# Five raw weight buffers in place of three, and a smaller scratch for software DMAs, in an fp32 encoder layer on one core

## The chip, the core and the metric

The kernel runs on one core of one Trainium2 chip. Its engines are TensorE (PE in the profile; PEld is its weight loads), VectorE (DVE), ScalarE (ACT), GpSimd (POOL) and SyncE (SP), which here only issues DMAs. Each engine works through its own queue in order and waits at semaphores. The metric is the device time of one execution in microseconds. Before the change the median of three runs is 819.6 us (819.17 to 819.94).

## The reference

One layer of an encoder, 512 tokens of width 1024, all in float32:

```python
D_MODEL = 1024; SEQ = 512; D_FF = 2752
def swiglu(h, w_gate, w_up, w_down):
    return (jax.nn.silu(h @ w_gate) * (h @ w_up)) @ w_down
...
    x = x + 0.5 * swiglu(rms_norm(x, ffn1_norm), ffn1_w_gate, ffn1_w_up, ffn1_w_down)
    h = rms_norm(x, mix_norm)
    u = h @ w_in
    ...
    f_out = fourier_mixer(u[..., :o0], fnet_w, fnet_b)
    a_out = gqa_attention(u[..., o0:o1], u[..., o1:o2], u[..., o2:], q_norm, k_norm)
    x = x + jnp.concatenate([f_out, a_out], axis=-1) @ w_out
    x = x + 0.5 * swiglu(rms_norm(x, ffn2_norm), ffn2_w_gate, ffn2_w_up, ffn2_w_down)
return rms_norm(x, final_norm)
```

The two feed-forward blocks (FFN1 and FFN2) hold most of the work: three weight matrices of 1024 x 2752 each. The mixer between them has a Fourier part and an attention part.

## The kernel before

**Arithmetic.** TensorE multiplies in fp32r, a rounded float32. To keep float32 accuracy each operand is split into a high part (a cast) and a low part (what the cast lost), and a product is three matmuls: high by high, high by low, low by high (`product`, L186). For weights the high part is cast by ScalarE (`weights`, L172; `both`, L391; `single`, L400) and the low part is a subtraction on VectorE (`lows`, L130), from the raw tile and the high part. A few low parts are made by GpSimd's software DMA, which adds the weights from memory onto the negated high part (`rest_by_dma`, L159 and L160).

**Tiles.** Activations stand transposed: eight tiles of 128 features by 512 tokens. The feed-forward width is cut into 21 chunks of 128 and a rest (`"t"`). A block is done in four groups of chunks (`GROUPS1`, `GROUPS2`). Gate and up of a chunk are computed in one of two ways. In the first group they are plain products (`gate`). In the others a 2 x 2 block scheme with seven products in place of eight is used (`seven`, with p, q and r as its PSUM banks); it needs sums of raw gate and up weights, which `prepare` makes: s12 and s34, four VectorE operations (`combine`, L406) of 128x512, cast and split afterwards as 128x1024. After gate and up of a group, `down` multiplies the group's activations (tile at) with the down weights for each of eight output tiles d (dn0_d_g: FFN 0 or 2, tile d, group g), and `residual` (L575) adds half of it to the residual stream gx. A group of six chunks gives 18 matmuls per d, one of two or three chunks with the rest some 8 to 11.

**Buffers.** Weights come from memory as raw tiles of 4 KB per partition. Down weights (`raw_tile`, L154), up weights of `prepare` (raw_u, L383) and the weights of the mixer share one tag "raw" in the pool `wp` (L92), which has three buffers. Gate weights of `prepare` (raw_g) have two buffers in another pool. A load can be issued when the last reader of the tile that had the buffer is done, and SyncE issues the loads in a fixed order, so a load that waits holds up those behind it.

**What sets the order.** On TensorE and SyncE the order inside the feed-forward blocks is that of the program (`in_order`). On VectorE, ScalarE and GpSimd it is set there by the framework's scheduler when the program is built: it simulates the program with its own costs, and so with the buffers that it has. In the mixer all engines follow a list written out by hand (`ORDER`). The profile's time has no part in any of this.

The lines that matter:

```python
def lows(lo, src, hi):                                             # L130
    nc.vector.tensor_tensor(out=lo, in0=src, in1=asf(hi), op=ALU.subtract)
def raw_tile(src, name, n=KD):                                     # L154
    raw = wp.tile([P, KD, P], F32, tag="raw", name=f"raw_{name}")
    nc.sync.dma_start(out=raw[:, :n, :], in_=src)
...
    u = wp.tile([P, KD * P], F32, tag="raw", name=f"raw_u{n_}_{j}")  # prepare
...
    def combine(out, a, b, op):                                    # L406
        nc.vector.tensor_tensor(out=out, in0=a, in1=b, op=op)
```

Of the kernel before, what the change touches and what calls it, by code (L numbers as in the profile page):

```python
# [88 lines left out]
def encoder(ctx, tc, A, out):  # L89
    nc = tc.nc  # L90
    cp = ctx.enter_context(tc.tile_pool(name="const", bufs=1))
    wp = ctx.enter_context(tc.tile_pool(name="weights", bufs=3))  # L92

    whole = cp.tile([P, FRONT + NS * KD * P + 2 * ROOM], F32R, name="ring")
    ring = whole[:, FRONT:]
# [1471 lines left out]
```

## Time and profile before

| | |
|---|---|
| median of three runs | 819.6 us |
| the profiled execution: span | 817.3 us |
| TensorE busy | 809.9 us, 99% |
| VectorE busy | 652.0 us, 80% |
| ScalarE busy | 503.5 us, 62% |
| GpSimd busy | 67.7 us, 8% |
| mean granted TensorE clock | 0.999 |
| moved by DMA | 99.75 MB, 122 GB/s |

The span is that of the profiled execution on the chip, from its first to its last instruction; a run's time is 2.3 us longer at the median, and no other time of that execution is recorded. Times of events are counted from the span's start. FFN1 runs from 0 to some 330, the mixer until some 485, FFN2 until some 810, and the final normalisation is the end. Rows of the timeline are: start, duration, engine, line, operation, what is written from what, shape, and in brackets the idle time before and what ended it. A row of a wait has the engine and line that waited, what it waited for, the total, the count and the longest. A matmul's duration contains its pipeline, so the pace of TensorE is read from starts.

### The profile page before, as it was taken

The numbers are of one execution on the slowest core, as the hardware profiler recorded it, in microseconds if no ns is written. First come the engines' busy times: TensorE is split into PE (matmuls) and PEld (weight loads), VectorE is DVE, ScalarE is ACT, GpSimd is POOL, SyncE is SP. The second block draws the span as 40 slices with busy tenths as digits, with TensorE's granted clock in tenths as the row PEclk, the third lists the DMA queues.
The fourth block names the chain that finished last, engine by engine and source line by source line (L and its number), as shares of the span: only waits on it lengthen the run. The fifth ranks groups of instructions, "written<-read, shape, count | busy, mean of one in ns | idle before, by whom it ended". The sixth has DMA issues, their size and how long they took to land.

```text
span 817.3 us, 13006 instructions
## 1 busy us (share of the span) xinstructions
PE 809.9 (99%) x4936; PEld 729.0 (89%) x4936; DVE 652.0 (80%) x1080; ACT 503.5 (62%) x870; POOL 67.7 (8%) x75
## 2 busy tenths in 40 slices
PE   9999999999999999999999999999999999999997
PEld 6888998899989998889998888899988998899987
DVE  7997997489956857799998578999955997489674
ACT  7883774167624735699998449557733674267462
POOL 0320000000000000221000003100100000000001
PEclk9999999999999999999999999999999999999999
DMA  7874553345443423442201236564443553345222
GB/s 258 199 176 165 146 133 91 123 130 168 85 142 96 126 69 117 130 149 65 66 26 52 79 105 144 128 191 140 132 116 115 154 140 84 129 130 146 59 78 103
DMA packets 37390, 99.75 MB, mean 122 GB/s; under 512 B 4432, under 2 KB 10576, under 8 KB 37328
## 3 DMA queue, kind: packets, MB, share of 16 engines
q1 hardware_dynamic: 27776, 82.61, 31.3%
q0 software_dynamic: 8832, 15.34, 11.1%
q10 hardware_dynamic: 720, 0.98, 0.3%
q8 instruction: 38, 0.62, 0.3%
q14 instruction: 24, 0.20, 0.1%
HBM read 93.41 MB, written 2.10 MB: 117 GB/s over the span
## 4 chain that ended last, share of the span: by engine, by line
PE 96%; DMA 1%; DVE 1%; ACT 1%; issue 0%; POOL 0%; POOLq 0%; DVEq 0%; ACTq 0%
PE dn L186 24%; PE r L436 12%; PE mix L186 8%; PE r L441 8%; PE gu L186 8%; PE q L436 4%; PE q L441 4%; PE r L432 4%; PE p L432 4%; PE q L432 4%; PE gu L740 3%; PE p L441 2%; PE mix L1234 2%; PE mix L1200 2%; PE mix L1038 1%; PE mix L1039 1%
## 5 line engine op out<-in xcount | busy, mean ns | idle before, releaser
L186 PE MATMUL dn<-at,ring 128*128 128x512 f32 x900 | 202.9, 380 | 0.4 <-DVE ring L130 0.4
L186 PEld LDWEIGHTS dn<-at,ring 128*128 128x128 f32 x900 | 168.0, 188 | 29.5 <-DVE ring L130 1.0
L441 PE MATMUL r<-rt,ring 128*128 128x256 f32 x560 | 154.3, 276 | 0.0
L436 PE MATMUL r<-rt,ring 128*128 128x256 f32 x840 | 147.1, 276 | 0.0
L436 PEld LDWEIGHTS r<-rt,ring 128*128 128x128 f32 x840 | 127.0, 188 | 1.6
L441 PEld LDWEIGHTS r<-rt,ring 128*128 128x128 f32 x560 | 105.1, 188 | 0.2
L391 ACT CAST ring<-s 128x1024 fp32r<-128x1024 f32 x70 | 73.6, 1051 | 35.5 <-PE r L436 16.5
L130 DVE TENSOR_TENSOR ring<-s,ring 128x1024 fp32r<-128x1024 f32 x70 | 85.3, 1218 | 12.5 <-ACT ring L391 10.3
L575 DVE SCALAR_TENSOR_TENSOR gx<-dn,gx 128x512 f32<-128x512 f32 x61 | 41.9, 688 | 62.0 <-PE dn L186 61.8
L172 ACT CAST ring<-raw_dn 128x768 fp32r<-128x768 f32 (+3 forms) x58 | 45.3, 784 | 70.5 <-PE dn L186 52.5
L441 PE MATMUL q<-rt,ring 128*128 128x256 f32 x280 | 77.0, 275 | 0.0
L160 POOL DMA_DIRECT2D ring<-in_wgu x38 | 32.9, 867 | 470.9 <-ACT u L450 358.0
L130 DVE TENSOR_TENSOR ring<-raw_dn,ring 128x768 fp32r<-128x768 f32 (+3 forms) x58 | 51.5, 891 | 9.2 <-ACT ring L172 5.1
L441 PEld LDWEIGHTS q<-rt,ring 128*128 128x128 f32 x280 | 52.6, 188 | 0.0
L130 DVE TENSOR_TENSOR ring<-raw_g,ring 128x1024 fp32r<-128x1024 f32 x35 | 42.7, 1220 | 10.0 <-PE p L432 9.6
L436 PE MATMUL q<-rt,ring 128*128 128x256 f32 x280 | 49.8, 277 | 0.0
L186 PE MATMUL gu<-ring 128*128 128x512 f32 x216 | 48.9, 381 | 0.0
L432 PE MATMUL r<-rt,ring 128*128 128x512 f32 x140 | 48.7, 384 | 0.0
L432 PE MATMUL q<-rt,ring 128*128 128x512 f32 x140 | 48.3, 382 | 0.0
L432 PE MATMUL p<-rt,ring 128*128 128x512 f32 x140 | 48.3, 382 | 0.0
L186 PEld LDWEIGHTS gu<-ring 128*128 128x128 f32 x216 | 40.4, 188 | 6.9
L391 ACT CAST ring<-raw_g 128x1024 fp32r<-128x1024 f32 x35 | 36.8, 1051 | 13.9 <-DMA raw_g<-in_wgu 10.9
(277 smaller groups left out, 1658.6 us busy)
## 6 DMA issues: line engine op xcount, KB each, us to landing
raw_g<-in_wgu SPq DMA_DIRECT2D x35, 512.0 KB, 3.8
raw_u<-in_wgu SPq DMA_DIRECT2D x35, 512.0 KB, 4.5
raw_dn<-in_wd SPq DMA_DIRECT2D x40, 384.0 KB, 3.2
ring<-in_wgu POOLq DMA_DIRECT2D x35, 256.0 KB, 4.3
raw_gu<-in_wgu SPq DMA_DIRECT2D x12, 512.0 KB, 3.4
raw_o<-in_wo SPq DMA_DIRECT2D x8, 512.0 KB, 3.5
raw_dn<-in_wd SPq DMA_DIRECT2D x8, 448.0 KB, 3.4
raw_wq<-in_wins SPq DMA_DIRECT2D x4, 512.0 KB, 3.5
```

Of the source, the lines that this page charges most:

```text
L130: nc.vector.tensor_tensor(out=lo, in0=src, in1=asf(hi), op=ALU.subtract)
L160: nc.gpsimd.dma_start(out=lo, in_=src, accum_op=ALU.add)
L172: nc.scalar.copy(hi[:, :n, :], raw[:, :n, :])
L186: nc.tensor.matmul(ps, a, b, start=first and b is mhi and a is whi, stop=last and a is wlo)
L391: nc.scalar.copy(hi, src)
L432: nc.tensor.matmul(turned(ps), whi[:, ks], turned(m), start=start, stop=False, skip_group_check=True)
L436: nc.tensor.matmul(ps[:, t], whi[:, ks], m[:, o * HALF :][:, t], start=start and o == 0, stop=False, skip_group_check=True,)
L441: nc.tensor.matmul(o, wlo[:, ks], m, start=False, stop=stop, skip_group_check=True)
L575: nc.vector.scalar_tensor_tensor(out=x[d][:, t], in0=ps[:, t], scalar=0.5, in1=x[d][:, t], op0=ALU.mult, op1=ALU.add)
L740: nc.tensor.matmul(turned(pss[c]), w[:, k % 2, c], turned(m[k]), start=k == 0 and m is hh and w is hi, stop=k == KD - 1 and w is lo,)
L1200: nc.tensor.transpose(pts[n][:, c * P : (c + 1) * P], prob[t, b, c][:, kc * P : (kc + 1) * P], ident)
L1234: nc.tensor.matmul(turned(outs[t, b]), w, turned(p), start=kc == 0 and i == 0, stop=kc == 3 and i == 1)
```

## The change

The pool of raw weight tiles gets five buffers in place of three, and the scratch that GpSimd's software DMAs use for their descriptors gets 8192 bytes per partition in place of 16384 (the value that holds where none is given):

```diff
@@ encoder
-    wp = ctx.enter_context(tc.tile_pool(name="weights", bufs=3))
+    wp = ctx.enter_context(tc.tile_pool(name="weights", bufs=5))
@@ kernel
-    nc = bacc.Bacc("TRN2", target_bir_lowering=False, num_devices=1)
+    nc = bacc.Bacc("TRN2", target_bir_lowering=False, num_devices=1, dynamic_dma_scratch_size=8192)
```

Two buffers of 4096 bytes take just the 8192 bytes that the scratch gives up. The scratch lies at the start of the memory, so the constant tiles between it and the raw buffers move down by 8192 bytes, and all above the raw buffers stays where it was.

On TensorE and GpSimd the instructions stand as before; SyncE's loads too, but for one at the start that is issued two places earlier. On VectorE and ScalarE the scheduler comes to another order. Three pieces of VectorE's, as a difference (- before, + now; the numbers at the end of a name tell tiles apart).

The first is in FFN1's second group, while TensorE does the down products of d = 1 to 4. raw_dn0_3 to raw_dn0_5 are the down weights for d = 3 to 5, whose low parts are made here; raw_u0_11 and raw_g0_11 are the weights of chunk 11, which the next group needs.

```order
 L130 TENSOR_TENSOR ring_61<-raw_dn0_3_1_1475,ring_61 128x768
 L575 SCALAR_TENSOR_TENSOR gx_69<-dn0_2_1_1449,gx_69 128x512
+L406 TENSOR_TENSOR s12_0_11_1608<-raw_u0_11_1605 128x512
+L406 TENSOR_TENSOR s34_0_11_1609<-raw_g0_11_1604,raw_u0_11_1605 128x512
 L130 TENSOR_TENSOR ring_61<-raw_dn0_4_1_1500,ring_61 128x768
+L406 TENSOR_TENSOR s12_0_11_1608<-s12_0_11_1608,raw_g0_11_1604 128x512
+L406 TENSOR_TENSOR s34_0_11_1609<-raw_g0_11_1604,s12_0_11_1608 128x512
 L575 SCALAR_TENSOR_TENSOR gx_69<-dn0_3_1_1474,gx_69 128x512
 L130 TENSOR_TENSOR ring_61<-raw_dn0_5_1_1526,ring_61 128x768
 L575 SCALAR_TENSOR_TENSOR gx_69<-dn0_4_1_1499,gx_69 128x512
-L406 TENSOR_TENSOR s12_0_11_1608<-raw_u0_11_1605 128x512
-L406 TENSOR_TENSOR s34_0_11_1609<-raw_g0_11_1604,raw_u0_11_1605 128x512
```

The sums of chunk 11 have moved from behind the low part of raw_dn0_5 to both sides of that of raw_dn0_4; all four stand ahead of raw_dn0_5 now. The same is done in FFN1's third group and in the second and third of FFN2.

The second is in FFN2's first group, where at2 is the activations' tile, whose free room also holds a low part of a down weight, and u2p a product of gate and up.

```order
 L130 TENSOR_TENSOR ring_61<-raw_dn2_3_0_5243,ring_61 128x256
-L406 TENSOR_TENSOR s12_2_3_5273<-raw_u2_3_5270 128x512
-L406 TENSOR_TENSOR s34_2_3_5274<-raw_g2_3_5269,raw_u2_3_5270 128x512
+L662 TENSOR_TENSOR u2p_5234<-g2p_5233,u2p_5234 128x512
+L406 TENSOR_TENSOR s34_2_3_5274<-raw_g2_3_5269,s12_2_3_5273 128x512
+L575 SCALAR_TENSOR_TENSOR gx_69<-dn2_1_0_5242,gx_69 128x512
+L130 TENSOR_TENSOR ring_61<-s12_2_3_5273,ring_61 128x1024
+L130 TENSOR_TENSOR at2_4887<-raw_dn2_4_0_5257,at2_4887 128x256
+L575 SCALAR_TENSOR_TENSOR gx_69<-dn2_2_0_5256,gx_69 128x512
 L130 TENSOR_TENSOR at2_4887<-u2p_5234,at2_4887 128x512
-L575 SCALAR_TENSOR_TENSOR gx_69<-dn2_1_0_5242,gx_69 128x512
-L130 TENSOR_TENSOR at2_4887<-raw_dn2_4_0_5257,at2_4887 128x256
```

Ahead of the low part of raw_dn2_4 stand now, beside what stood there, the last sum of s34 for chunk 3 and the 1024-wide low part of its s12; the low part of u2p has moved behind it.

The third is a little later in the same group.

```order
 L575 SCALAR_TENSOR_TENSOR gx_69<-dn2_3_0_5278,gx_69 128x512
-L130 TENSOR_TENSOR ring_61<-s12_2_3_5273,ring_61 128x1024
+L406 TENSOR_TENSOR s12_2_4_5355<-raw_u2_4_5352 128x512
+L130 TENSOR_TENSOR ring_61<-s34_2_3_5274,ring_61 128x1024
 L130 TENSOR_TENSOR ring_61<-raw_dn2_6_0_5294,ring_61 128x256
 L575 SCALAR_TENSOR_TENSOR gx_69<-dn2_4_0_5293,gx_69 128x512
-L130 TENSOR_TENSOR ring_61<-s34_2_3_5274,ring_61 128x1024
 L130 TENSOR_TENSOR at2_4887<-raw_dn2_7_0_5309,at2_4887 128x256
```

The 1024-wide low part of s12 is gone from here, that of s34 has moved ahead of the low part of raw_dn2_6, and with it a sum that reads the up weights of chunk 4.

Other rows moved are the token weights of the last three down tiles at the end of FFN2 (L548, L549: half of a raw tile, split, for products that have tokens as rows), which stand earlier; a sum and a low part in FFN1's first group, which stand ahead of the low part of raw_dn0_5; and the low parts of raw_dn_1, which stand a few rows earlier in four groups.

## The prediction

> **What bounds the kernel now.** I read the page from the top: the busy times, the chain that ended last, then the waits of each engine.
>
> ```profile
> span 817.3 us, 13006 instructions
> PE 809.9 (99%) x4936; PEld 729.0 (89%) x4936; DVE 652.0 (80%) x1080; ACT 503.5 (62%) x870; POOL 67.7 (8%) x75
> PE 96%; DMA 1%; DVE 1%; ACT 1%; issue 0%; POOL 0%; POOLq 0%; DVEq 0%; ACTq 0%
> ```
>
> TensorE (PE) is busy for 99% of the span and carries 96% of the chain. More buffers remove no matmul, so the change can win only what TensorE waits. The waits (engine, line and what was waited for: us in total, times, longest):
>
> ```profile
> PE dn L186 <- DVE ring L130: 0.4, 1, 0.4
> ...
> SPq L154 <- DVE ring L130: 203.7, 46, 13.3
> ```
>
> SyncE's queue stands 203.7 us behind raw buffers that are not free yet, which is what two more of them relax. But that waiting is hidden: TensorE itself waits for a low part in one place that this view shows. The large number is no gain; the small one is. Where that wait comes from stands in the chain (start, us, what):
>
> ```profile
> 147.31 0.97 DVE ring L130
> 148.30 4.86 DMA raw_u<-in_wgu
> 153.79 0.68 DVE s L406
> 154.48 0.88 DVE ring L130
> 155.40 7.75 PE dn L186 x34
> ```
>
> The buffer for the up weights of chunk 11 (raw_u) is freed by the low part of raw_dn5 at 147.31; the load takes until 153.2; VectorE's sums (L406) wait for it, and the low part of raw_dn6 stands behind them on VectorE's queue. That ends at 154.48+0.88 = 155.36, and the matmul that reads it starts at 155.40. How long TensorE stood there is read from the starts:
>
> ```profile
> 139.39 0.96 DVE L130 TENSOR_TENSOR ring<-raw_dn,ring 128x768 fp32r<-128x768 f32 x1
> 153.19 0.69 DVE L406 TENSOR_TENSOR s<-raw_u 128x512 f32<-128x512 f32 x1 [1.87 <-DMA raw_u<-in_wgu]
> ...
> 142.73 12.28 PE L186 MATMUL dn<-at,ring 128*128 128x512 f32 x55
> ```
>
> A 512-wide matmul starts 0.22 us after the one before (further down, three take 530.10 to 530.76). 55 of them from 142.73 put the next at 154.83; it came at 155.40. The wait is 0.57 us.
>
> **The change part by part.** *The stall that goes.* With five buffers that load needs only the low part of raw_dn3, which ends at 139.39+0.96 = 140.35, eight microseconds earlier, and the low part of raw_dn6 no longer has an L406 ahead of it that waits. The term is **-0.57**, and it cannot be more.
>
> *What is late next.* The scheduler has used the earlier load. In four places (the second and third group of each FFN) it puts two of the L406 sums ahead of the low part of raw_dn4, where nothing waited. That low part is due two blocks of 18 matmuls (18 x 0.22 = 3.96 us each) before 154.83, at 146.91. To end 0.04 before that it must start by 146.91-0.04-0.96 = 145.91, and the first of two L406, 0.60 apart (153.19 to 153.79), by 144.71. From an issue at 140.40 that leaves 4.3 us. Before, these rows give the time from the issue of that load to the L406 that waits for it:
>
> ```profile
> 148.30 0.33 SPq L383 DMA_DIRECT2D raw_u<-in_wgu  x1
> 237.49 0.33 SPq L383 DMA_DIRECT2D raw_u<-in_wgu  x1
> 612.01 0.33 SPq L383 DMA_DIRECT2D raw_u<-in_wgu  x1
> 700.51 0.33 SPq L383 DMA_DIRECT2D raw_u<-in_wgu  x1
> ...
> 241.37 0.69 DVE L406 TENSOR_TENSOR s<-raw_u 128x512 f32<-128x512 f32 x1 [0.86 <-DMA raw_u<-in_wgu]
> 615.70 0.69 DVE L406 TENSOR_TENSOR s<-raw_u 128x512 f32<-128x512 f32 x1 [0.67 <-DMA raw_u<-in_wgu]
> 703.97 0.69 DVE L406 TENSOR_TENSOR s<-raw_u 128x512 f32<-128x512 f32 x1 [0.43 <-DMA raw_u<-in_wgu]
> ```
>
> They are 4.89, 3.88, 3.69 and 3.46 us. Three fit into 4.3, one misses by 0.6. The four places together cost between 0 (all in time) and 4 x 0.6 = 2.4 (all as slow as the first). I take **+0.3**, half of one miss, since three of the four rows lie on the side of no wait. Behind the waiting L406 stand, on VectorE, the low part of raw_dn4, two more sums and a residual; only the first of them has TensorE waiting for it.
>
> *The first group of FFN2.* Here it is VectorE that has nothing to spare (its busy time is the fourth figure of the first row, of 20 us):
>
> ```profile
> 520.00:540.00 20.00, 20.00 (x98) 16.85 (x97) 19.55 (x33) 9.19 (x16) 0.92 (x1) 1.00 0.58 189
> ...
> 523.52 1.23 DVE L130 TENSOR_TENSOR ring<-raw_g,ring 128x1024 fp32r<-128x1024 f32 x1 [0.42 <-ACT ring L391]
> 524.66 0.68 DVE L660 TENSOR_TENSOR u2p<-gu,rb 128x512 f32<-128x512 f32 x1
> 532.40 1.21 DVE L130 TENSOR_TENSOR ring<-s,ring 128x1024 fp32r<-128x1024 f32 x1
> 533.53 0.41 DVE L130 TENSOR_TENSOR ring<-raw_dn,ring 128x256 fp32r<-128x256 f32 x1
> 533.87 0.68 DVE L575 SCALAR_TENSOR_TENSOR gx<-dn,gx 128x512 f32<-128x512 f32 x1
> ...
> 530.10 0.82 PE L186 MATMUL dn<-at 128*128 128x512 f32 x3
> 530.76 0.38 PE L533 MATMUL dn<-at,wt 128*128 128x512 f32 x1
> 532.96 1.54 PE L186 MATMUL dn<-at,ring 128*128 128x512 f32 x6
> 534.34 0.39 PE L533 MATMUL dn<-at,wt 128*128 128x512 f32 x1
> 535.45 1.11 PE L186 MATMUL dn<-at 128*128 128x512 f32 x3
> 536.40 0.39 PE L533 MATMUL dn<-at,wt 128*128 128x512 f32 x1
> ```
>
> I laid the new sequence of VectorE out from 524.66, with the start-to-start times of these rows: 1.13 for a 1024-wide low part (532.40 to 533.53), 0.33 for a 256-wide one (533.53 to 533.87), 0.60 for a 512-wide operation. Ahead of the low part of raw_dn4 now stand eight 512-wide operations (four L406 sums, L660, L662, two residuals), the low part of raw_dn3 and the 1024-wide one of s12. So it starts at 524.66 + 8 x 0.60 + 0.33 + 1.13 = 530.92 and ends, with 0.41, at 531.33. The third matmul of the row at 530.10 reads it, due at 530.54: TensorE waits 531.33+0.04-530.54 = 0.83.
>
> Then come a residual, the low part of at from u2p, that of raw_dn5, a residual, the first L406 of chunk 4 and the 1024-wide low part of s34, before the low part of raw_dn6: 530.92 + 0.33 + 4 x 0.60 + 0.33 + 1.13 = 535.11, end 535.52. Its reader is the sixth matmul of the row at 532.96, due at 534.06 and, moved by the first wait, at 534.89: another 0.67. The low part of raw_dn7, at 536.4, is then in time. Against 1.50 stands what the stretch loses today: 535.45 to 536.40 is 0.95 where three matmuls take 0.66, and 532.96 to 534.34 is 1.38 where six take 1.32, together 0.35. Net **+1.15**. The bounds: -0.35, if VectorE gets through so much faster that nothing waits and today's loss goes too, and +2.3, if the up weights of chunk 3 or 4, for which the walk assumes no wait, land a microsecond later (each is issued just behind its gate weights, and the slowest row above is a microsecond over the other three). I take the walk, since its durations are those of this very stretch.
>
> *Other places that move.* In FFN1's first group a sum and a 1024-wide low part go ahead of the low part of raw_dn5:
>
> ```profile
> 58.61 0.55 DVE L130 TENSOR_TENSOR at<-raw_dn,at 128x384 fp32r<-128x384 f32 x1
> 63.69 1.21 DVE L130 TENSOR_TENSOR ring<-s,ring 128x1024 fp32r<-128x1024 f32 x1
> 64.82 0.55 DVE L130 TENSOR_TENSOR ring<-raw_dn,ring 128x384 fp32r<-128x384 f32 x1
> ...
> 65.06 2.14 PE L186 MATMUL dn<-at,ring 128*128 128x512 f32 x9
> ```
>
> The load is freed at 59.16 and at the slowest 4.89 lands at 64.05, where the queue reaches its sum at 63.69. The low part, with 0.60 more ahead of it and 0.36 of wait, ends at 64.82+0.96+0.55 = 66.33; the ninth matmul of the last row reads it at 66.82. **0**, with half a microsecond of cover; without it some 0.5. Near the end the token weights (L548, L549) of three raw tiles move forward, into idle time of VectorE:
>
> ```profile
> 775.62 1.09 DVE L130 TENSOR_TENSOR ring<-raw_dn,ring 128x896 fp32r<-128x896 f32 x1 [4.03 <-PE r L432]
> ```
>
> Two of about 1.09 fit into the 4.03 us ahead of this row. **0**; if the second load came late, about one such operation, 1.1. The order on TensorE and GpSimd is the same as before.
>
> *The smaller scratch.* It concerns GpSimd's own DMAs:
>
> ```profile
> q0 software_dynamic: 8832, 15.34, 11.1%
> L160 POOL DMA_DIRECT2D ring<-in_wgu x38 | 32.9, 867 | 470.9 <-ACT u L450 358.0
> ```
>
> The group waits 470.9 us for its inputs, and the queue takes 11.1% of the DMA engines' time, so a wait for room would have much cover: **0**. If a load of it had to wait for the one before, that is of the order of one 867 ns issue and hidden as well. By the Trainium skill, "DMA: Bandwidth & Descriptors", section "SWDGE vs HWDGE vs iDMA", GpSimd writes these descriptors into rings that lie in a part of SBUF kept for them, and only one such queue is allocated; a shorter ring could so make GpSimd wait, which is why the third rival below has the ring in it. No trace here shows a full ring.
>
> What also moves is the constant tiles' address, by 8192 bytes. No row prices it. If it changed a matmul by 1 ns either way, 4936 of them make 4.9 us; the nearest row, the pitch of 0.22 across tiles at all addresses, speaks for nothing.
>
> The sum is on the profiled span of 817.3 us, 2.3 below the median of 819.6, which I carry over: 819.6 - 0.57 + 0.3 + 1.15 = 820.5.
>
> **The rivals.** *First: VectorE keeps up in FFN2's first group.* The up weights' sums fill today's idle slots there and the two low parts come in time: 819.6-0.57-0.35 = 818.7, up to 819.0 if today's 0.35 stays. For it: the walk's lateness is some 0.8 of 20 us. Against it: 19.55 of 20 us busy.
>
> *Second, slower: the up weights land late, everywhere.* The L406 ahead of raw_dn4 waits, with TensorE behind it, in all four places, once a load takes over 4.3 us from its issue: 820.5-0.3+2.4 = 822.6; with a late load in FFN2's first group as well, 823.7. For it: five buffers let more loads run at the same time, and one row took 4.89 as it is. Against it: the other three.
>
> *Third: the address or the ring matters.* Matmuls or software DMAs change by a nanosecond each: 815 or 825. Nothing in the profile speaks for it.
>
> *Fourth: nothing that TensorE sees changes* (the loads run ahead, the scheduler's order costs as much as it gains): 819.6.
>
> **How the numbers follow.** A measurement of this kernel tells a difference from about 0.2%, 1.6 us: below 818.0 is faster, above 821.2 slower. The forecast 820.5 has 0.42, its own range 819.6 to 821.6; the first rival 0.20; the second 0.22; the third 0.08, half each way; the fourth 0.08. Slower: the second rival, 0.04 of the third and a sixth of the forecast, 0.33. Faster: 0.04 of the third and 0.03 of the first, if more goes there than its rows show, 0.07. The same: 0.60. The range 818.5 to 822.8 holds the forecast, the first, the fourth and most of the second.
>
> **What would show it.** In the profile after: no wait of TensorE at about 155, with the raw_u load issued at about 140 and not 148; in the four places the L406 just ahead of the low part of raw_dn4 waits for raw_u, and TensorE at most once by about 0.6; VectorE's low part of raw_dn4 at about 531 in FFN2's first group with TensorE waiting 0.8 for it, and 0.7 for that of raw_dn6; SyncE's waits for L130 far below 203.7. I am wrong if TensorE's waits between 520 and 540 stay at 0.35 or less, if the waits in the four places exceed 1 us, or if matmuls take another time.

## The result

The changed kernel takes 821.68 us at the median of seven runs (821.46 to 823.06), the kernel before 819.94 beside it (818.79 to 820.34). The ratio is 1.0028, with a 95% interval of 1.0019 to 1.0038: slower by about a quarter of a per cent. That ratio is 2.3 us; the two medians are 1.7 us apart. The forecast was 820.5, with a range of 818.5 to 822.8. In every run whose span is on record the time is 1.7 to 1.9 us above the span, so the profile before, of 817.3, belongs to an execution of some 819.1, faster than its median, and the two profiles lie further apart (2.6 us) than the medians.

The page of the changed kernel, its first lines and the chain that ended last:

```profile
span 819.9 us, 12990 instructions
PE 810.9 (99%) x4936; PEld 729.5 (89%) x4936; DVE 652.0 (80%) x1080; ACT 502.8 (61%) x870; POOL 67.7 (8%) x75
PE 85%; DMA 5%; ACT 3%; DVE 3%; issue 2%; POOL 0%; SPq 0%; POOLq 0%; DVEq 0%; ACTq 0%
```

The work is the same to a microsecond, but the chain now runs for 5% through loads and for 3% each through ScalarE and VectorE, where it ran for 96% through TensorE. TensorE's waits and SyncE's two longest (us in total, times, longest):

```profile
PE dn L186 <- DVE at L130: 0.9, 1, 0.9
...
PE r L432 <- ACT u L489: 0.5, 1, 0.5
PE dn L186 <- DVE ring L130: 0.4, 1, 0.4
...
PE q L432 <- ACT p L450: 0.2, 1, 0.2
...
SPq L383 <- DVE g L445: 147.6, 13, 20.1
SPq L154 <- DVE ring L130: 144.1, 33, 16.4
```

SyncE waits less in the last row, 144.1 us for 203.7, as the change intends. But its waiting has moved rather than gone: the row above it, for loads of gate and up weights (L383), was 100.9 before, and all of SyncE's waits together are 746 us in both profiles. TensorE waits in more places. To see all of it, I matched the 4936 matmuls of both traces in order and took the difference of their starts. These are its steps; each includes what is said of a restart further down, and steps of under 0.1 us are left out:

| where (us of the profile before) | step of the difference, us | what TensorE waits for |
|---|---|---|
| 5 and 25, the start | +0.21, +0.17 | first casts, first normalisation |
| 107 | +0.5 | ScalarE's copy p (L450), new |
| 155 | -0.7 | the low part of raw_dn6, gone |
| 272 and 276 | +0.6, +0.4 | ScalarE's copies u and p (L489, L450) |
| 530 to 537 | +1.5 | VectorE's low parts of raw_dn4 and raw_dn6 |
| 754 | -0.2 | ScalarE's copy |
| end | +2.6 | (the two spans differ by 2.6) |

The wait that the prediction took away is gone, and the largest that it added is there. But a good microsecond comes from places that it had put at nothing: ScalarE, in FFN1. There the chain reads (start, us, what), first at 98 and then at 264 us:

```profile
98.39 6.96 DMA raw_dn<-in_wd
...
105.37 0.03 ACT ring L172
...
106.11 1.04 ACT ring L391
107.16 0.27 ACT u L450
107.43 0.52 ACT ring L400
107.95 0.28 ACT p L450
...
108.27 0.48 PE q L432
...
264.69 5.74 DMA raw_dn<-in_wd
...
270.45 0.83 ACT ring L172
271.28 0.47 ACT ring L391
271.75 0.39 issue
272.14 0.36 ACT u L489
```

A raw_dn tile is loaded, ScalarE stands at the cast (L172) until it lands, and the copies that free TensorE's PSUM banks (L450, L489) stand behind the cast on the same queue. ScalarE's idle time before those casts, and one more cast a little later, in the kernel changed; then the second of them before:

```profile
105.37 0.84 ACT L172 CAST ring<-raw_dn 128x768 fp32r<-128x768 f32 x1 [1.95 <-DMA raw_dn<-in_wd]
...
270.45 0.83 ACT L172 CAST ring<-raw_dn 128x768 fp32r<-128x768 f32 x1 [2.40 <-DMA raw_dn<-in_wd]
...
272.93 0.82 ACT L172 CAST ring<-raw_dn 128x768 fp32r<-128x768 f32 x1
```

```profile
269.72 0.84 ACT L172 CAST ring<-raw_dn 128x768 fp32r<-128x768 f32 x1 [1.76 <-DMA raw_dn<-in_wd]
```

The first of them (raw_dn1) is a cast that the scheduler moved forward: it was at 110.18. The second (raw_dn0) stood there before, but its load lands later now: 5.74 us after its issue at 264.69, before 3.9 after one at 265.77. The third, at 272.93, is raw_dn1 of that group, also moved forward (it was at 278.67). It waits for no load; it stands ahead of the copies with its own length, and the wait at 276 follows.

### The profile page after: what moved, and what is told of

It reads as the page before. It is cut to its first block, busy times and chain, and to the rows that moved or that the text cites. A ratio compares the mean times of both kernels' runs of the same rounds, so it can differ in the third digit from the quotient of the medians.

```text
span 819.9 us, 12990 instructions
## 1 busy us (share of the span) xinstructions
PE 810.9 (99%) x4936; PEld 729.5 (89%) x4936; DVE 652.0 (80%) x1080; ACT 502.8 (61%) x870; POOL 67.7 (8%) x75
## 4 chain that ended last, share of the span: by engine, by line
PE 85%; DMA 5%; ACT 3%; DVE 3%; issue 2%; POOL 0%; SPq 0%; POOLq 0%; DVEq 0%; ACTq 0%
PE dn L186 24%; PE r L436 11%; PE mix L186 8%; PE r L441 7%; PE q L432 4%; PE q L441 4%; PE gu L186 4%; PE q L436 3%; PE r L432 3%; PE p L432 3%; DMA raw_dn<-in_wd 2%; PE p L441 2%; PE mix L1234 2%; PE mix L1200 2%; DMA rawt<-in_wdt 1%
## 5 line engine op out<-in xcount | busy, mean ns | idle before, releaser
L172 ACT CAST ring<-raw_dn 128x768 fp32r<-128x768 f32 (+3 forms) x58 | 45.2, 783 | 75.1 <-PE dn L186 64.5
L441 PEld LDWEIGHTS q<-rt,ring 128*128 128x128 f32 x280 | 52.6, 188 | 0.0
L436 PEld LDWEIGHTS q<-rt,ring 128*128 128x128 f32 x280 | 42.3, 188 | 1.2
```

The source lines that it names most:

```text
L172: nc.scalar.copy(hi[:, :n, :], raw[:, :n, :])
L436: nc.tensor.matmul(ps[:, t], whi[:, ks], m[:, o * HALF :][:, t], start=start and o == 0, stop=False, skip_group_check=True,)
L441: nc.tensor.matmul(o, wlo[:, ks], m, start=False, stop=stop, skip_group_check=True)
```

## The experiments

My theory after this reading: the buffers and the scratch cost nothing by themselves. What costs is the order that the scheduler made with them on VectorE and ScalarE, in FFN2's first group and at the casts of raw_dn1 in FFN1. The rivals: the moved addresses or the shorter ring cost something; or more loads in flight make each land later, whatever the order.

For most runs the order of VectorE and ScalarE is held fast outside the mixer, from a table of instruction names, by edges that set the order of issue on one engine and add no wait:

```diff
@@ kernel
         encoder(tc, aps, out)
+        keep(nc, tc)
...
+def keep(nc, tc):
+    info = mybir.DependencyInfo(mybir.DependencyClass.NoSync, mybir.DependencyReason.DATA)
+    for names in KEEP.values():
+        names = [f"I-{n}" for n in names.split()]
+        for a, b in zip(names, names[1:]):
+            tc.add_manual_dep(nc.get_inst_by_name(b), a, info, reason="order")
+KEEP = {("DVE", 0): "87 112 116 113 ...", ...}
```

The runs differ in the table alone where nothing else is said. Each ratio below is to the kernel before, run beside it (medians of 819.3 to 819.4).

### The scratch alone

```diff
@@ kernel (of the kernel before: three buffers)
-    nc = bacc.Bacc("TRN2", target_bir_lowering=False, num_devices=1)
+    nc = bacc.Bacc("TRN2", target_bir_lowering=False, num_devices=1, dynamic_dma_scratch_size=8192)
```

> Three raw buffers as before, and the scratch of 8192 bytes: the constant tiles move down by 8192 bytes and the software ring is halved, while the order on every engine is that of before. Theory (all of the change's time comes from the order on VectorE and ScalarE and from earlier loads): the same as before, span 817.3 within 0.5 us, ratio 1.000. Rival (the addresses or the shorter ring cost something): above before by up to 2.6 us, ratio up to 1.003, spread evenly over the matmuls or with longer GpSimd issues (L160 above 867 ns).

819.65 us, ratio 1.0004 (0.9995 to 1.0013): no difference that the measurement shows. GpSimd's software DMAs take what they took, and wait for their inputs as long as before (470.9):

```profile
L160 POOL DMA_DIRECT2D ring<-in_wgu x38 | 32.9, 867 | 471.0 <-ACT u L450 364.3 <-DVE u L496 52.0 <-DVE ring L130 17.2
```

The span, 818.2, is 0.9 above that of the profile before, and I had allowed 0.5. One place makes all of it, the wait at 155 that five buffers take away; elsewhere the starts of the matmuls keep their distance from those before within 0.2 us, so neither the addresses nor the ring show a price. The wait at 155 is larger here than in the profile before, since the load took 5.82 us and not 4.86:

```profile
PE dn L186 <- DVE ring L130: 1.4, 1, 1.4
...
148.27 5.82 DMA raw_u<-in_wgu
```

So a wait for a load is not one number: in this place it was 0.57 in one execution and 1.53 in another (from the starts of the matmuls).

### The order of before with five buffers

> Five buffers and the small scratch, with the instructions of VectorE and ScalarE outside the mixer held in the order of before. Theory (the order costs): the waits at 107, 272, 277, 531 and 536 us of the profile after are gone, today's wait at 155 is gone too because the load is early; span 816.6 to 817.6, 2.3 to 3.3 below the changed kernel's 819.9, ratio to before 0.999 to 1.000. Rival (more loads in flight make each land later, whatever the order): raw_dn still lands in 4.0 us, waits move to other casts, span 818.5 or more.

819.26 us, ratio 1.0005 (0.9995 to 1.0014), span 817.1. With the order gone, the loss is gone. The wait at 155 is gone too; what is left is 0.30 us at 271, and 0.30 and 0.19 in FFN2's first group. So two more buffers by themselves bring nothing that the measurement shows. The starts show what cancels: against the profile before, 0.7 us is won at 155 and 0.2 at 754, and 0.3 is lost at 271 and 0.35 in FFN2's first group. A second time, beside a later experiment:

> The five buffers with the order of before once more, as the run to compare the held load with: raw_dn0 of FFN1's last group lands 5.2 to 6.2 us after its issue, TensorE waits 0 to 1.0 us at 271, median 819.0 to 819.6.

819.89 us, ratio 1.0007 (0.9995 to 1.0019), span 818.1; the wait at 271 was 0.65 and the load of raw_dn0 took 5.73 us, and FFN2's first group lost 0.6. The median is 0.3 above what I expected, the ratio agrees.

### Each part undone

FFN2's first group in the order of before, the rest as in the change:

> The changed kernel with the order of before on VectorE and ScalarE in FFN2's first group alone (520 to 545 us). Theory: the waits of 1.08 and 0.57 us there shrink to before's 0.3, the rest stays: span 818.3 to 818.6, 1.3 to 1.6 below 819.9. Rival (TensorE waits there for a load, not for VectorE's order): below by less than 0.5.

820.50 us, ratio 1.0014 (1.0004 to 1.0025), span 818.0: 1.9 below the changed kernel's profile. More than I expected, and not only from that place: in this execution the waits at 107 and 272 did not come (0.19 was left at 275). The runs spread from 818.77 to 822.6; how often those waits come is not shown, since one execution is profiled, but here they did not come though the order at both places is the change's.

The casts of raw_dn1 in the order of before, the rest as in the change:

> The changed kernel with the order of before on VectorE and ScalarE where the casts of raw_dn1 were moved in FFN1 (103 to 118 and 271 to 286 us). Theory: the waits of TensorE for ScalarE's copies at 107.7, 271.8 and 276.7 us, 0.4, 0.66 and 0.22 us, go with the casts that no longer stand ahead of the copies: span 818.6 to 819.0, 0.9 to 1.3 below 819.9. Rival (the copies are late for another reason, as the cast at 270.4 that is not moved waits for its load too): below by less than 0.5.

820.60 us, ratio 1.0017 (1.0008 to 1.0026), span 819.0, as expected. Of the waits at 107, 271 and 276 none is left but the 0.11 at 271 that the kernel before has too, and FFN2's stand:

```profile
PE dn L186 <- DVE at L130: 1.1, 1, 1.1
...
PE dn L186 <- DVE ring L130: 0.4, 1, 0.4
```

### Each part alone

FFN2's first group in the order of the change, the rest as before:

> Five buffers with the order of before everywhere but in FFN2's first group (520 to 545 us). Theory: TensorE waits there 1.6 to 1.9 us, as in the changed kernel, against 0.5 with the order of before: median 820.4 to 820.8, 1.1 to 1.5 above 819.3. Rival (a part of the wait there is passed on from earlier delays): under 0.6 above.

821.05 us, ratio 1.0022 (1.0012 to 1.0033): a little above the range that I expected, and 1.2 to 1.8 above the two runs with the order of before, the theory's side. It is most of the loss. In the starts TensorE loses 2.0 us in this group, with the order of before 0.7 and 1.0, so some 1.0 to 1.25 is the order's. This profile also has a wait of 1.00 at 271, where the order is that of before.

The casts of raw_dn1 in the order of the change, the rest as before:

> Five buffers with the order of before everywhere on VectorE and ScalarE but at the two places in FFN1 where the cast of raw_dn1 was moved forward (103 to 118 and 271 to 286 us). Theory (a cast that waits for its load stands ahead of the copies that TensorE waits for, and how long varies with the load): slower than the run with the order of before (median 819.3) by 0.5 to 1.3 us, median 819.8 to 820.6, and wider spread than that run. Rival (these waits came from the one profiled execution): 819.3 within 0.3.

820.13 us, ratio 1.0010 (1.0000 to 1.0020), runs from 818.86 to 822.2. At 271 TensorE waited 0.77 and at 276 0.30 us. With the same moves on ScalarE alone:

> Five buffers, VectorE in the order of before everywhere, ScalarE in the order of the change at the two places of raw_dn1 in FFN1 alone. Theory (it is ScalarE's cast ahead of its copies that costs): waits of TensorE for ScalarE's copies near 271 and 276 us of 0.3 to 1.0 together, as with both engines' moves; median 819.6 to 820.6. Rival (VectorE's moved low part costs): as with the order of before, no more than its wait at 271.

820.66 us, ratio 1.0020 (1.0011 to 1.0029), with 0.55 at 271 and 0.29 at 276. The wait at 276 is ScalarE's order: VectorE had that of before, and 0.29 stands beside 0.30. But the wait at 271 came with the order of before as well, with 0.30, 0.65 and, beside FFN2's moves, 1.00 us, where the two kernels with three buffers and that order had 0.11 and nothing. Only the one at 276 belongs to the moved cast alone. The one at 107 came in the changed kernel's profile, where the load of raw_dn1 took 6.96 us, and in none of the three other profiles with that cast moved, where it took 5.9, 6.25 and 6.5. So the rival has a share: with five buffers the load of raw_dn0 lands later.

### One load held back

Five buffers and the order of before, and one more edge, a wait this time, between SyncE's load and ScalarE's cast:

```diff
@@ keep
+    held = mybir.DependencyInfo(mybir.DependencyClass.Sync, mybir.DependencyReason.DATA)
+    tc.add_manual_dep(nc.get_inst_by_name("I-3053"), "I-3021", held, reason="raw_dn0_1_3 behind the cast of raw_dn0_0_3")
```

> The five buffers with the order of before, and one load held back: raw_dn1 of FFN1's last group is issued only when the cast of raw_dn0 is done (some 270 us), where the other five-buffer runs issue three such loads within 1.2 us. Theory (several loads in flight share the DMA engines, so the first of them lands later though it is issued earlier): raw_dn0 lands 3.9 to 4.6 us after its issue, not 5.4 to 6.1, and TensorE's wait at 271 is below 0.15 us. Rival (it lands late for the gate and up weights ahead of it alone): 5.4 us or more as before, wait of 0.3 to 1.0.

818.98 us, ratio 0.9998 (0.9989 to 1.0008), span 817.0. The loads' issue and the cast that waits, in this run, and in the first run with the order of before:

```profile
263.03 0.33 SPq L383 DMA_DIRECT2D raw_g<-in_wgu  x1
...
263.89 7.14 SPq L154 DMA_DIRECT2D raw_dn<-in_wd  x3
...
268.98 0.84 ACT L172 CAST ring<-raw_dn 128x768 fp32r<-128x768 f32 x1 [1.73 <-DMA raw_dn<-in_wd]
```

```profile
262.94 0.33 SPq L383 DMA_DIRECT2D raw_g<-in_wgu  x1
...
263.80 1.51 SPq L154 DMA_DIRECT2D raw_dn<-in_wd  x3
...
269.20 0.84 ACT L172 CAST ring<-raw_dn 128x768 fp32r<-128x768 f32 x1 [2.04 <-DMA raw_dn<-in_wd]
```

The three raw_dn loads are issued over 7.14 us here and over 1.51 there. The first lands 5.1 us after its issue, not the 3.9 to 4.6 that I expected, and not 5.4 or more; TensorE does not wait at 271. But the cast can start as early without the held load. In the run with raw_dn1's casts undone:

```profile
263.35 0.33 SPq L383 DMA_DIRECT2D raw_g<-in_wgu  x1
...
264.21 1.51 SPq L154 DMA_DIRECT2D raw_dn<-in_wd  x3
...
269.30 0.84 ACT L172 CAST ring<-raw_dn 128x768 fp32r<-128x768 f32 x1 [1.73 <-DMA raw_dn<-in_wd]
```

Counted from the gate weights' issue (raw_g, a microsecond ahead) the cast starts after 5.95 us in the run with the held load, 5.98 with three buffers (263.74 to 269.72), and 5.7 to 7.0 in the eight other runs that issue three raw_dn at once and have this cast in its place; in two of them, that of FFN2's first group undone (5.72) and the one above (5.95), it is no later than with the load held back. So this time alone does not tell the two explanations apart.

The DMA packets in the traces do. A raw_dn load is 128 packets of 3072 bytes. When raw_dn0 landed, 128 such packets had ended in the run with the held load and in the three with three buffers, and 191 to 284 in the nine that issue three raw_dn at once: packets of the loads behind it had run before it was done. From the end of the 128th packet to the landing it took 0.3 to 0.4 us in the first four and 0.6 to 1.4 us in the nine. So each of the two explanations holds a part: the load stands behind the gate and up weights whenever it is issued, so that issuing it 1.1 us earlier gives nothing, and the two loads behind it take some 0.2 to 1.1 us from it, an estimate from these differences. One execution each, so the size is rough.

### A version that beats both, with five buffers and with three

Seventeen moves by hand in the table of before: casts and low parts of raw_dn0 and raw_dn1 behind the next copies, the low part of raw_dn6 ahead of the L406 that wait for raw_u (the four places of the prediction), and in FFN2's first group the low parts of raw_dn6 and raw_dn7 ahead of the 1024-wide ones, with that of u2p behind them. Once with the change's buffers and scratch:

> Five buffers, the order of before with moves by hand: casts and low parts of raw_dn0 and raw_dn1 behind the next copies; the low part of raw_dn6 ahead of the L406 that wait for raw_u; in FFN2's first group the low parts of raw_dn6 and raw_dn7 ahead of the 1024-wide ones, that of u2p behind them. Theory (all waits of TensorE inside the feed-forward blocks come from the order): no wait over 0.1 us between 100 and 330 and between 490 and 800; span 816.2 to 816.8, median 818.2 to 818.9, ratio to before 0.9987 to 0.9995. Rival (loads, not the order, set what is left): same as before within 0.3.

817.89 us, ratio 0.9982 (0.9973 to 0.9991), span 816.4; once with three buffers and the scratch of 16384:

> Three buffers and the scratch of 16384 bytes as before, with the same moves by hand. Theory (two more buffers give nothing that the order does not): the wait at 155 goes though the load is as late as before; within 0.4 us of the five buffers with that order, ratio to before 0.9987 to 1.000. Rival (the buffers are needed: later casts hold three buffers longer, and loads come late): new waits of TensorE for raw_dn or raw_u, 0.5 us or more above the five buffers.

817.76 us, ratio 0.9986 (0.9977 to 0.9995), span 817.8. TensorE's waits, with five and with three:

```profile
PE busy L685 <- PEq L1550: 0.8, 1, 0.8
PE gu L740 <- ACT ring L726: 0.3, 1, 0.3
```

```profile
PE busy L685 <- PEq L1550: 0.8, 1, 0.8
PE gu L740 <- ACT ring L726: 0.6, 1, 0.6
```

Both rows are from the first six microseconds; no wait over 0.1 us comes after them, in either. With three buffers the up weights of chunk 11 come as late as ever, and it costs nothing, since only the sums that need them stand behind:

```profile
150.24 0.33 SPq L383 DMA_DIRECT2D raw_u<-in_wgu  x1
...
155.95 0.69 DVE L406 TENSOR_TENSOR s<-raw_u 128x512 f32<-128x512 f32 x1 [1.77 <-DMA raw_u<-in_wgu]
```

The two spans differ by 1.4 us, and that arises before 10 us (last section). The wait was a matter of order; the buffers were one way round it, and not needed.

## Why the prediction was right or wrong

**What bounds the kernel: right.** The chain and the waits said that 203.7 us of SyncE's waiting are hidden and that the change can win only what TensorE waits. That row fell to 144.1 us and nothing was won by it; all of SyncE's waits together stayed at 746 us.

**The stall that goes: right, -0.57 forecast, -0.7 measured.** The difference is the restart (last section).

**The four places with L406 ahead of raw_dn4: +0.3 forecast, 0 measured.** From the issue to the L406 it took 3.64 us in the first (below), and 3.66, 3.52 and 3.79 in the others, all under the 4.3 that were left. The slow 4.89 that I took half of came from one execution of one place. It was priced on the right side, and too high.

```profile
141.16 0.33 SPq L383 DMA_DIRECT2D raw_u<-in_wgu  x1
...
144.80 0.69 DVE L406 TENSOR_TENSOR s<-raw_u 128x512 f32<-128x512 f32 x1 [0.62 <-DMA raw_u<-in_wgu]
```

**FFN2's first group: the mechanism right, +1.15 forecast, +1.5 measured.** The rows that answer to the walk:

```profile
525.05 1.23 DVE L130 TENSOR_TENSOR ring<-raw_g,ring 128x1024 fp32r<-128x1024 f32 x1 [0.61 <-ACT ring L391]
526.19 0.68 DVE L406 TENSOR_TENSOR s<-raw_u 128x512 f32<-128x512 f32 x1
532.47 0.41 DVE L130 TENSOR_TENSOR at<-raw_dn,at 128x256 fp32r<-128x256 f32 x1
536.67 0.41 DVE L130 TENSOR_TENSOR ring<-raw_dn,ring 128x256 fp32r<-128x256 f32 x1
...
531.42 0.62 PE L186 MATMUL dn<-at 128*128 128x512 f32 x2
532.93 0.49 PE L186 MATMUL dn<-at 128*128 128x512 f32 x1 [0.90 <-DVE at L130]
533.26 0.39 PE L533 MATMUL dn<-at,wt 128*128 128x512 f32 x1
537.14 0.49 PE L186 MATMUL dn<-at,ring 128*128 128x512 f32 x1 [0.39 <-DVE ring L130]
```

From the operation behind the gate weights' low part to the low part of raw_dn4 the walk said 6.26 us, and it is 532.47-526.19 = 6.28; from there to raw_dn6 it said 4.19, and it is 4.20. What was mis-sized is its start. All this stands 1.32 us later than in the profile before by what TensorE had lost until then, but the gate weights' low part starts 1.53 later (525.05 for 523.52), since ScalarE's cast of them waits for a load that comes 0.2 later against TensorE; with three buffers that load took 3.4 to 3.5 us, with five 3.6 to 4.1. So the first wait is 1.08 and not 0.83 us, the second 0.57 for 0.67, and two restarts of 0.11 come on top: 1.87, against the 0.35 that the stretch lost before.

**"Other places that move: 0": wrong, and it is the step that failed.** I had walked VectorE's queue with TensorE's due times for the low parts, and had seen that raw_dn1's low parts moved a few rows; the sum has nothing for them, without a reason, and nothing for their casts on ScalarE, which moved too. The price is not that of the casts: it is that of the copies behind them on ScalarE. Before, the copy p at 107 ended 0.4 us ahead of its matmul, that at 276 as well, and the copy u at 271 just in time. Which load the cast waits for, how long that takes to land, and who stands behind the cast: that was the question that I had asked for VectorE, and not for ScalarE. Of the 1.5 us that TensorE lost for ScalarE's copies, 0.9 (at 107 and 276) goes with the moved casts, and 0.6 (at 271) with a cast that did not move and a load that lands later, which the forecast did not price either. The size of the moved casts alone is loosely known: 820.13 and 820.66 lie 0.2 to 1.4 us above the two runs with the order of before, and the intervals overlap.

**Scratch, ring and addresses: 0 forecast, 0 measured** (ratio 1.0004). The rule of the Trainium skill that I cited ("DMA: Bandwidth & Descriptors", section "SWDGE vs HWDGE vs iDMA") gives a way in which the ring could matter; no run here shows it: GpSimd's issues took 867 ns with half of it.

**The rivals.** The first (VectorE keeps up in FFN2's first group) is refuted by the run with that part alone. The second had the right side, slower, and the wrong place: loads did come late, but in front of ScalarE's casts and not of the L406. The third is refuted. The fourth is what five buffers are with the order of before.

The sum by steps would be -0.7 + 0 + 1.5 + 1.5 - 0.2 + 0.4 = 2.5, and 2.6 with the small steps, the difference of the spans; the forecast had -0.57 + 0.3 + 1.15 = 0.9. Of the 1.7 that are missing, what ScalarE's copies cost is the larger part. The chance that I gave to slower was 0.33. That 821.68 lies inside the stated range is in part luck: its upper end was there for the second rival, whose waits did not come, and the forecast's own range, 819.6 to 821.6, misses it.

## What to carry to other kernels

More buffers changed three things here: when loads are issued, how long a load takes to land with others behind it, and, where a scheduler sets the order by its own costs, the order of everything. Compare the orders, and for every instruction that moves forward, above all one that waits for a load, look at the whole queue behind it on its engine, on each engine: what counts is the slack of the shortest-lived waiter there (here a copy that frees a PSUM bank), not that of the instruction itself. The waiting time of the load queue said nothing here of what buffers are worth; a wait on the engine that bounds did, and then moving the work behind the late load to another place did more than making the load early.

## What I had not expected of the hardware

**An early issue need not be an early landing.** The median from issue to landing of the 40 raw_dn loads of 384 KB was 3.2 us in the three profiles with three buffers and 3.9 to 4.4 in the ten with five; before and in the changed kernel:

```profile
raw_dn<-in_wd SPq DMA_DIRECT2D x40, 384.0 KB, 3.2
```

```profile
raw_dn<-in_wd SPq DMA_DIRECT2D x40, 384.0 KB, 4.0
```

The Trainium skill, "DMA: Bandwidth & Descriptors", section "Issuing engines are not separate DMA queues", says that all DMAs run on the same 16 engines and interleave; the trace agrees for loads that SyncE alone issues, with the 191 to 284 packets above, where the load itself has 128.

**A wait costs more than it lasts.** The matmul that has waited is followed by the next after 0.33 us and not 0.22, in each wait of 0.2 us or more in the feed-forward blocks of these profiles (532.93 to 533.26 above): 0.11 us on top.

**TensorE's first matmuls can run at half speed, and that differs from run to run.** With the same order, in the first ten microseconds of the two hand-ordered kernels, five buffers first:

```profile
5.12 5.18 PE L740 MATMUL gu<-ring 128*128 128x512 f32 x20 [0.34 <-ACT ring L726]
```

```profile
5.34 4.99 PE L740 MATMUL gu<-ring 128*128 128x512 f32 x13 [0.56 <-ACT ring L726]
```

20 matmuls start in the one and 13 in the other. In the second, the starts up to 8.9 us stand 427 ns apart, as those of the warm-up matmuls before 4 us do, and then 220; at 10 us it is 1.6 us behind the first, and the spans differ by 1.4. The granted clock of these slices shows 1.00 in both. The Trainium skill, "TensorE: Matmul & The Clock Gate", Part 1, says that an idle array runs at half clock until a free-running window of some 3.4 us has been busy, so that the number of slow matmuls varies from run to run, and gives 426.7 ns for this size; the trace agrees, with 427 ns. At 10 us the twelve other profiles lie within 0.7 us of each other, and this one 1.6 behind the last of them. Its execution took 819.56 us, as two more of that kernel's eleven did within 0.2, where the other eight took 817.2 to 818.2; that those two started in the same way is not shown. It is a reason not to compare two spans without the starts of their matmuls.
